# A macaron block in fp32 on one core: weight sums of the second feed-forward made during the mixer and kept in DRAM, buffers given by due time, and the head in one list

## The chip, the cores and the metric

The kernel runs on one core of one Trainium2 chip. The metric is the device time of one execution in microseconds (us): 2007.45 us as the median of three runs (2005.02 to 2007.62) for the kernel before.

## What is computed

For 256 tokens of width 2048, all in fp32, three sublayers stand in a row, each between two norms and with a residual:

```
...
for l in range(DEPTH):
    f = _swiglu(_rmsnorm(h, ln_ffn1_pre[l]), ffn1_gate[l], ffn1_up[l], ffn1_down[l])
    h = h + MACARON_WEIGHT * _rmsnorm(f, ln_ffn1_post[l])
    mx = _hybrid_mixer(_rmsnorm(h, ln_mix_pre[l]), w_in[l], ...)
    h = h + _rmsnorm(mx, ln_mix_post[l])
    f = _swiglu(_rmsnorm(h, ln_ffn2_pre[l]), ffn2_gate[l], ffn2_up[l], ffn2_down[l])
    h = h + MACARON_WEIGHT * _rmsnorm(f, ln_ffn2_post[l])
...
```

`_swiglu` is `(silu(x @ w_gate) * (x @ w_up)) @ w_down` with a hidden width of 5632. The mixer multiplies by `w_in`, runs a linear recurrence (RWKV-7) over 16 heads and a windowed pooling beside it, and joins both by gated products with `w_proj_a`, `w_proj_b` and `w_out`.

## The kernel before

**Matmuls.** A fp32 number is split into a high part H (a cast by ScalarE, ACT) and the rest L (a subtraction by VectorE, DVE). `mm3` (L332 to L334) makes each product as three matmuls of 128x128 by 128x512. Weights come by SP's queue in tiles of 128x1024 fp32 (512 KB, two k-tiles of 512 columns) into four `w32` buffers; `two` (L386, L396 in `fetch`, L308, L309) writes the halves into a ring of five `wH`, `wL` pairs. All other large tiles are "units" of 4 KB a partition, 33 of them in one pool (`s.unit`, NUNITS): activations, sums, scratch.

**Quads.** In the feed-forwards two outputs of 512 columns are made together, `f` and `l` (a block of gate and of up, or two column blocks of down), for the two halves of the tokens. For two k-tiles that is 2x2 by 2x2, and `seven` does it either as two plain pairs (one `f` and one `l`, 12 matmuls each) or as one quad: Strassen's seven products in Winograd's form, 21 matmuls. A quad needs four sums of weights (t13, two tiles, in L622; t2 in L627; t4 in L631) and the split of seven weight tiles (L639, L644). In the letter lists GATE_UP and DOWN, `f` and `l` are pairs, `q` is a quad whose sums are all made on DVE, and `Q` one whose t13 is made by an adding DMA of GpSimd (POOL): `begin` loads two tiles by SP, `adding` (L617) adds the third, and DVE makes t2 and t4 alone. The five PE steps of a quad are at the end of `quad`. GATE_UP has 17 q, 24 Q, 78 f and l pairs; DOWN 11 q and 7 Q. Both feed-forwards use the same lists.

**The planner.** `Plan` holds the steps of a feed-forward as nodes of an engine with a duration, dependencies, and buffers ("tokens") taken and released. `solve` gives each a due time from PE's order, simulates the engines with fixed costs, and returns one order, in which the instructions are issued by hand (`run`, inside `manual_schedule`). A unit is taken by whichever node is ready first.

**The head.** The first product starts cold: `head` writes its own order for PE, ACT, DVE and SP inside a `manual_schedule` of its own (transposes of x, splits of the first weights, L309). The plan of the first feed-forward is a second such list. It begins with `normed`, which joins H and L of the activations (L1249).

**The mixer.** Only PE has an order by hand there; the other engines are ordered by the compiler's scheduler, by place in the program, with weight splits boosted ahead. It opens with plain products by `tok_g`: each loops over k-tiles, four at a time (three where it is 288 columns wide). The opening is one group of 288 columns and five of 512 (two for the pooling, then k, v and r of the first half of the heads). Then two recurrences, one for each half, are woven with more such products ("fill": the other half's k, v, r, the gates, `w_proj_b`). `across` moves the results into place with 16 small POOL transfers each (L1071). In the opening, `uT2` holds 8 units, `R` 15, `lq` and `sgb0` one each.

Of the kernel before, what the change touches and what calls it, by code (L numbers as in the profile page):

```python
# [10 lines left out]
F32 = mybir.dt.float32  # L11
# [6 lines left out]
P = 128  # L18
# [26 lines left out]
DOWN = ((0, "fffffQfffQfffflfqllQlllqqllQlqllflll", 0),  # L45
        (2, "fQqffqfqllffQqflffqfQfqlqf", TRAIL))
OUT = ((0, "", 0), (1, "fffqfq" "qlqlll", 0), (3, "", TRAIL))
GATE_UP = ["", "fffflQlfqfllll",
           "fqqflQQQfll", "flflQfqqQfll", "flqQfffqQlll",
           "flfQfQqfqlll", "flffQQqqQll", "fQfQfQQfllll",  # L50
           "ffqqQflQqll", "flffQQqfQlll", "fQfqqlQlflfl"]
SUMS = (2, 2, 1)
LATE, KEPT = 7, 5
# [30 lines left out]
class Node:  # L84
    def __init__(s, eng, dur, fn, deps, take, rel, due, size, ahead, spare, lat, early):
        s.eng, s.dur, s.fn, s.due, s.size = eng, dur, fn, due, size
        s.early = early
        s.ahead, s.spare, s.lat = ahead, spare, LAT[eng] if lat is None else lat
        s.deps = [d for d in deps if d]
        s.take, s.rel = take, rel  # L90
        s.start = s.end = s.free = None
        for r in rel:
            r.left += 1


class Plan:


    def __init__(s):
        s.fifos = {r: [] for r in FIFO}  # L100
        s.nodes, s.last, s.chain, s.clk = [], None, {}, 0.0
        s.units, s.inserts = [0.0] * UNITS["out"], []
        s.begin = s.pe(BEFORE, lambda: None)
# [39 lines left out]
    def solve(s):  # L143
# [15 lines left out]
        busy = dict.fromkeys(LAT, 0.0)  # L159
# [3 lines left out]
        ready = {}  # L163

# [26 lines left out]
        while len(order) < len(s.nodes):  # L191
# [15 lines left out]
            when(n)  # L207
            front[n.eng].remove(n)
# [23 lines left out]
class Block:  # L232
    def __init__(s, tc, ctx):
        s.tc = tc
        s.nc = nc = tc.nc
        E = ctx.enter_context
        s.n = 0
        s.nxt = None
        s.late, s.after, s.chain_pow = [], [], None
        s.own_stats = False  # L240
        s.plan, s.ready = Plan(), {}
# [36 lines left out]

    def run(s):

        E = mybir.EngineType
# [245 lines left out]
    def seven(s, wf, cf, wl, cl, at, dep, KT, need, sm, order, ev_f, ev_l, used, trail=0):  # L527
# [4 lines left out]
        n = order.lower().count("q")  # L532
# [5 lines left out]
        early = "l" in order[:order.lower().rfind("q") + 1].lower()  # L538
# [4 lines left out]
        if n and early and trail:  # L543
            cut["l1"] = std - 2 * order[:order.lower().rfind("q")].count("l")
        if n and trail:
            cut["l0"] = std - 2 * order[:order.lower().rfind("q")].count("l")
# [44 lines left out]
        def quad(q, far):  # L591
            k = 2 * q
            v, x = {}, {}
# [52 lines left out]
            if far:  # L646
                n13 = p.op("SP", 0.8, begin, take=[k13], size=0.52, ahead=FETCH)
                n13 = p.op("POOL", 1.0, adding, [n13], size=0.94, lat=FAR)
# [15 lines left out]
            n2 = p.op("DVE", one, t2, [n13, ld[0]], [k24] * far, [ka, k13])  # L664
            lb, rb = half("b", 1, [ld[3]], [kb])
            n4 = p.op("DVE", one, t4, [n2, ld[3]], (), [kb])
# [79 lines left out]
        for c in order:  # L746
            if c in "qQ":
                last["q"] = quad(nq, c == "Q")
# [45 lines left out]
    def head(s, w, c0, KT, do, keep, xs):  # L794
# [10 lines left out]
        E = mybir.EngineType  # L805
        with s.tc.manual_schedule(engines={E.PE, E.Activation, E.DVE, E.SP}):
# [33 lines left out]
    def tok_g(s, w, c0, at, KT, evac, cw=512):  # L840
# [3 lines left out]
        for k0 in range(0, KT, n):  # L844
            for k, wH, wL in s.load_w(w, k0, min(n, KT - k0), c0, cw):
                xH, xL = at(k)
                for h in range(2):
                    s.mm3(pss[h], xH[:, h * P:h * P + P], xL[:, h * P:h * P + P], wH, wL,
                          k == 0, k == KT - 1)
                    yield 3 * MM * cw / 512  # L850
        s.prime()
        with s.tc.high_priority(offset=BOOST):
            for h in range(2):
                evac(h, pss[h])

# [224 lines left out]
    def ffn(s, wg, wu, wd, uT, rs, gpost, resid, emit, reload, xs=None):  # L1080
# [3 lines left out]
        nb = NKF // 4  # L1084
        one = cost("DVE", 512)
# [23 lines left out]
        p.units = UNITS["first" if xs else "ffn"]  # L1109
        rsd = p.begin  # L1110
# [54 lines left out]
        su, sud, suk = [None] * 6, {}, []  # L1165

        def need(q):
            j = q // 2
            if j not in sud:
                sud[j], k = s.sums(nT, nTd, j, su, nq=SUMS[j], x32=nx[j])  # L1170
# [3 lines left out]
        for b in range(1, nb):  # L1174
# [9 lines left out]
            def ev_l(h, d, ap, use, b=b, silu=silu, mul=mul, k1=k1):  # L1184
                g, mine = silu[h]

                def mult():
# [8 lines left out]
                    GATE_UP[b], ev_f, ev_l, {})  # L1196
            carry(b, [mul[0], mul[1]], k1)
        p.release([p.last], nTk + suk)
        s.post(wd, s.T_at(hT), NKF, gpost, 0.5, resid, emit, reload, hT, hTd, sm, DOWN, hTk, hx)
# [35 lines left out]
    def normed(s, uT, rb, rows, uTk):  # L1235
# [6 lines left out]
        for i in range(len(uT)):  # L1242
# [13 lines left out]
            def low(x=x, nH=nH, nL=nL):  # L1256
# [8 lines left out]
                             () if i < len(SUMS) else [kx]))  # L1265
            toks += kT
            if i < len(SUMS):
# [239 lines left out]
    def mixer(s, prm, uT, rs, resid, emit, gpost, reload):  # L1507
# [150 lines left out]

        with s.tc.manual_schedule(engines={mybir.EngineType.PE}):
# [3 lines left out]
            for hf in range(2):  # L1663
                weave(chain(hf), fill)
# [396 lines left out]
def kernel(tc, x, ln_ffn1_pre, ln_ffn1_post, ffn1_gate, ffn1_up, ffn1_down,  # L2061
# [11 lines left out]
    with ExitStack() as ctx:  # L2073
# [48 lines left out]
        s.mixer(prm, uT2, rs2, at_tok(h1), emit2, ln_mix_post[0],  # L2122
                load_to(h1, lambda h: hsp[0, h]))

        def emit(h, c, ap, node, t):
# [3 lines left out]
              at_tok(h2), emit, load_to(h2, lambda h: hsp[1, h]))  # L2129
# [33 lines left out]
```

## Time and profile before

| | |
|---|---|
| median of three runs | 2007.45 us (2005.02 to 2007.62) |
| the profiled execution | 2005.37 us |
| its span | 2003.7 us |
| PE busy | 1990.0 us (99%) |
| weight loads of PE | 1644.7 us (82%) |
| DVE busy | 1813.6 us (91%) |
| ACT busy | 1224.3 us (61%) |
| POOL busy | 410.0 us (20%) |
| HBM read, written | 445.45 MB, 8.39 MB |

The span is from the first to the last instruction. Busy time is the time in which an engine has an instruction of its own running. By the stages of the trace the first feed-forward ends near 700 us, the mixer's opening lies from 717 to 843 us, its recurrences end near 1180 us, and the second feed-forward begins near 1290 us (the product with `w_out` lies between). A row of a view by stage gives the stage, its length, then for PE, PEld (weight loads), DVE, ACT and POOL the busy time with the number of instructions, then the clock granted to PE, the busy share of the 16 DMA engines and the GB/s moved.

### The profile page before, as it was taken

Reading aid. Unit: us, or ns where it says so; the run is one execution under the profiler, and the core shown is the slowest. Engines: PE = TensorE matmul, PEld = TensorE weight load, DVE = VectorE, ACT = ScalarE, POOL = GpSimd, SP = SyncE. Lnnn points to the kernel's source line nnn. Section 1 sums busy time; section 2 is a strip of 40 time slices with the busy share of each in tenths; the row PEclk is TensorE's granted clock in tenths of the full one; section 3 lists DMA queues with packets and bytes.
Section 4 is the critical chain, followed back from the end, with each engine's and each line's share of the span. In section 5 each row is a group of like instructions: output and inputs, shape, how many; then the busy total and the mean of one; then the engine's idle time right before and its main releaser. Section 6 shows DMA issues by size and latency. Waiting matters only on the chain.

```text
span 2003.7 us, 29050 instructions
## 1 busy us (share of the span) xinstructions
PE 1990.0 (99%) x9903; PEld 1644.7 (82%) x9903; DVE 1813.6 (91%) x2462; ACT 1224.3 (61%) x1631; POOL 410.0 (20%) x747
## 2 busy tenths in 40 slices
PE   9999999999999999999999999999999999999998
PEld 7888888888888888888788788888888888888886
DVE  6999999999999957799689678989999999999997
ACT  7566665676665566685466434575666656666563
POOL 2222231323000113412320111012222313230000
PEclk9999999999999999999999999999999999999999
DMA  9788798878778767757556547768888988876784
GB/s 341 226 268 270 216 304 271 254 238 257 211 229 272 264 191 210 206 174 219 147 168 189 169 158 262 263 226 276 265 269 254 276 259 244 258 242 207 232 284 158
DMA packets 253941, 472.36 MB, mean 236 GB/s; under 512 B 27363, under 2 KB 30816, under 8 KB 253792
## 3 DMA queue, kind: packets, MB, share of 16 engines
q1 hardware_dynamic: 213984, 400.89, 60.4%
q0 software_dynamic: 39520, 69.08, 15.3%
q8 instruction: 78, 1.28, 0.3%
q10 hardware_dynamic: 288, 0.52, 0.1%
q14 instruction: 71, 0.58, 0.1%
HBM read 445.45 MB, written 8.39 MB: 227 GB/s over the span
## 4 chain that ended last, share of the span: by engine, by line
PE 93%; DVE 3%; DMA 2%; issue 1%; ACT 0%; SPq 0%; DVEq 0%; POOLq 0%; POOL 0%; ACTq 0%
PE mm L332 25%; PE mm L334 24%; PE mm L333 24%; PE ms L333 5%; PE ms L334 5%; PE ms L332 5%; DMA w<-in_ffn_down_dram 1%; DVE wL L644 1%; PE tr L939 1%; DVE wL L396 1%; DMA w<-in_w_out_dram 0%; PE pA L1881 0%; DVE t L622 0%; PE mc L901 0%; DVE t L627 0%
## 5 line engine op out<-in xcount | busy, mean ns | idle before, releaser
L332 PE MATMUL mm<-wH,xH 128*128 128x512 f32 (+1 forms) x2008 | 784.3, 391 | 2.0 <-ACT wH L386 1.5
L334 PE MATMUL mm<-wH,xL 128*128 128x512 f32 (+1 forms) x2008 | 779.4, 388 | 0.1
L333 PE MATMUL mm<-wL,xH 128*128 128x512 f32 (+1 forms) x2008 | 779.3, 388 | 0.1
L332 PEld LDWEIGHTS mm<-wH,xH 128*128 128x128 f32 x2008 | 377.2, 188 | 80.9 <-ACT wH L386 1.9
L334 PEld LDWEIGHTS mm<-wH,xL 128*128 128x128 f32 x2008 | 377.0, 188 | 78.7 <-DVE xL L957 1.1
L333 PEld LDWEIGHTS mm<-wL,xH 128*128 128x128 f32 x2008 | 377.3, 188 | 75.7 <-DVE wL L309 0.4
L639 ACT CAST wH<-t 128x1024 fp32r<-128x1024 f32 x244 | 257.1, 1055 | 221.2 <-PE mm L334 121.0
L386 ACT CAST wH<-w 128x1024 fp32r<-128x1024 f32 x293 | 302.8, 1053 | 128.6 <-PE mm L334 100.8
L396 DVE TENSOR_TENSOR wL<-w,wH 128x1024 fp32r<-128x1024 f32 x293 | 351.9, 1227 | 13.8 <-ACT wH L386 12.5
L644 DVE TENSOR_TENSOR wL<-t,wH 128x1024 fp32r<-128x1024 f32 x244 | 295.7, 1234 | 10.9 <-ACT wH L639 10.2
L309 DVE TENSOR_TENSOR wL<-w,wH 128x1024 fp32r<-128x1024 f32 (+2 forms) x184 | 217.5, 1190 | 84.6 <-ACT wH L308 83.2
L308 ACT CAST wH<-w 128x1024 fp32r<-128x1024 f32 (+2 forms) x184 | 188.8, 1030 | 167.0 <-PE mm L334 147.5
L639 ACT CAST wH<-w 128x1024 fp32r<-128x1024 f32 x244 | 200.1, 837 | 109.7 <-PE mm L334 75.1
L982 POOL DMA_DIRECT2D x<-T x352 | 180.6, 608 | 389.6 <-DVE T L965 76.1
L644 DVE TENSOR_TENSOR wL<-w,wH 128x1024 fp32r<-128x1024 f32 x244 | 231.6, 966 | 0.9 <-ACT wH L639 0.9
L333 PE MATMUL ms<-wL,sH 128*128 128x512 f32 x312 | 121.5, 389 | 0.2 <-DVE wL L644 0.2
L332 PE MATMUL ms<-wH,sH 128*128 128x512 f32 x312 | 121.4, 389 | 0.0
L334 PE MATMUL ms<-wH,sL 128*128 128x512 f32 x312 | 121.4, 389 | 0.0
L617 POOL DMA_DIRECT2D t<-in_ffn_up_dram x48 | 59.8, 1256 | 230.8 <-DMA t<-in_ffn_up_dram 56.1
L631 DVE TENSOR_TENSOR t<-w,t 128x512 f32<-128x512 f32 x122 | 85.5, 701 | 0.5 <-DMA w<-in_ffn_down_dram 0.2
L627 DVE TENSOR_TENSOR t<-w,t 128x512 f32<-128x512 f32 x122 | 85.3, 700 | 0.3 <-DMA w<-in_ffn_down_dram 0.3
L622 DVE TENSOR_TENSOR t<-w,w 128x1024 f32<-128x1024 f32 x60 | 73.8, 1231 | 2.8 <-DMA w<-in_ffn_down_dram 2.8
(353 smaller groups left out, 2312.4 us busy)
## 6 DMA issues: line engine op xcount, KB each, us to landing
w<-in_w_in_dram SPq DMA_DIRECT2D x128, 512.0 KB, 4.3
w<-in_ffn_down_dram SPq DMA_DIRECT2D x104, 512.0 KB, 6.5
w<-in_ffn_up_dram SPq DMA_DIRECT2D x94, 512.0 KB, 6.0
w<-in_ffn_gate_dram SPq DMA_DIRECT2D x92, 512.0 KB, 6.6
w<-in_ffn_gate_dram SPq DMA_DIRECT2D x168, 256.0 KB, 5.5
w<-in_ffn_down_dram SPq DMA_DIRECT2D x130, 256.0 KB, 4.9
w<-in_ffn_up_dram SPq DMA_DIRECT2D x116, 256.0 KB, 5.9
t<-in_ffn_up_dram POOLq DMA_DIRECT2D x48, 512.0 KB, 8.4
```

What stands on the lines that cost most here:

```text
L308: s.nc.scalar.copy(vH, v)
L309: s.nc.vector.tensor_tensor(out=vL, in0=v, in1=vH.bitcast(F32), op=ALU.subtract)
L332: nc.tensor.matmul(ps, aH, bH, start=start, stop=False, skip_group_check=seeded)
L333: nc.tensor.matmul(ps, aH, bL, start=False, stop=False, skip_group_check=seeded)
L334: nc.tensor.matmul(ps, aL, bH, start=False, stop=stop, skip_group_check=seeded)
L386: nc.scalar.copy(x["H"], x["v"])
L396: nc.vector.tensor_tensor(out=x["L"], in0=x["v"], in1=x["H"].bitcast(F32), op=ALU.subtract)
L627: V.tensor_tensor(out=v["t24"][:, 0], in0=v["a"][:, 0], in1=v["t13"][:, 1], op=ALU.add)
L631: V.tensor_tensor(out=v["t24"][:, 1], in0=v["b"][:, 1], in1=v["t24"][:, 0], op=ALU.add)
L639: nc.scalar.copy(H, src)
L644: V.tensor_tensor(out=L, in0=src, in1=H.bitcast(F32), op=ALU.subtract)
L982: nc.gpsimd.dma_start(out=x[0][q * 32:q * 32 + 32, i], in_=src[i * 32:i * 32 + 32, q])
```

## The change

1. **Sums made in the mixer.** The second feed-forward has lists of its own, GATE_UP2 (17 q, 8 Q, 23 of a new letter P, 64 pairs) and DOWN2 (9 q, 9 Q): 66 quads in place of 59. For each P, `premakes` loads four weight tiles into two units, makes t13, t2 and t4 with three DVE adds into a third unit and in place, and stores them to a DRAM tile by two POOL transfers. In `tok_g` one such job is taken after the k-tiles 4, 8 and 12 of a product, in the mixer's opening and during the second recurrence (PRE_AT). In the second feed-forward a P loads its two tiles of sums by SP (`bring`) in place of making them.
2. **Buffers by due time.** In `solve`, a node that takes units leaves free as many as the nodes due before it still need (`kept_for`). The lists of the first feed-forward are written anew for it, with the same number of quads (18 q and 23 Q in gate and up, 11 q and 7 Q in down).
3. **Head in one list.** `head` leaves its `manual_schedule` open and `run` goes on in it, with POOL among the listed engines from the start; the plan counts DVE as taken for its first 5.5 us and ACT for 4.5 us (TAKEN).

```
+GATE_UP2 = ["", "fPllfPfPqfll",
+    "flffPqPlfqll", "fqqPllqPffl", "fPfqPlPqlfl",
+    "fqfqPQflPll", "fflqQQPQfll", "fPqPllQPffl",
+    "fqfqlQQfPll", "flPPflqPqfl", "fPlqQPPlffl"]
+DOWN2 = ((0, "ffffffQfffflQqflllfqQlqlllQllQlfflll", 0),
+    (2, "fqffqQflqflQflqqqfffflQfQf", TRAIL))
+TAKEN = dict(DVE=5.5, ACT=4.5)
+PRE = 0
+PRE_AT = ((4, 8, 12), (), (4, 8, 12))
...
-        busy = dict.fromkeys(LAT, 0.0)
+        busy = {**dict.fromkeys(LAT, 0.0), **s.taken}
...
+        def kept_for(n):
+            c = 0
+            for m in takers:
+                if m.due >= n.due or c > NUNITS:
+                    break
+                c += m.units
+            return c
...
+            aside = kept_for(n) if any("unit" in k.res for k in n.take) else 0
...
-                    u, i = free[k.res[1]], HOLD if r == "ring" else SPARE
+                    u = free[k.res[1]]
+                    i = max(aside + (r == "ring"), HOLD if r == "ring" else SPARE)
...
-                at = free[r][i] if len(free[r]) > i else 1e18
+                j = i + aside * (r == "unit")
+                at = free[r][j] if len(free[r]) > j else 1e18
...
-        with s.tc.manual_schedule(engines={E.PE, E.Activation, E.DVE, E.SP, E.Pool}):
+        with s.open or s.listed():
+            s.open = None
             for n in s.plan.solve():
...
+            def bring(i):
+                v[("t13", "t24")[i]] = s.unit((P, 2, 512), F32, ("t13", "t24")[i])
+                nc.sync.dma_start(out=v[("t13", "t24")[i]], in_=made(q)[:, i])
+            if ready_made:
+                n13, n4 = [p.op("SP", 0.4, lambda i=i: bring(i), take=[(k13, k24)[i]], size=0.52,
+                                ahead=FETCH) for i in range(2)]
+            elif far:
...
+            if not ready_made:
+                n2 = p.op("DVE", one, t2, [n13, ld[0]], [k24] * far, [ka, k13])
...
+            if not ready_made:
+                n4 = p.op("DVE", one, t4, [n2, ld[3]], (), [kb])
...
-        with s.tc.manual_schedule(engines={E.PE, E.Activation, E.DVE, E.SP}):
+        stack = ExitStack()
+        stack.enter_context(s.listed())
+        with stack:
...
+            s.open = stack.pop_all()
...
+            if k0 in s.pre_at:
+                with s.tc.high_priority(offset=-PRE):
+                    next(s.jobs, None)
...
+    def premakes(s, wg, wu):
...
+                k = 2 * q
+                out = s.made[b, q] = s.dp.tile([P, 2, 2, 512], F32, tag=f"made{b}_{q}",
+                                               name=f"made{b}_{q}")
+                x, y, t = [s.unit((P, 2, 512), F32, n_) for n_ in ("ma", "mb", "mt")]
+                for i in range(2):
+                    for v, w in ((x, (wg, wu)[i]), (y, (wu, wg)[i])):
+                        nc.sync.dma_start(out=v[:, i], in_=w[(k + i) * P:(k + i + 1) * P,
+                                                             b * 512:b * 512 + 512])
+                V = nc.vector
+                V.tensor_tensor(out=t, in0=x, in1=y[:, :1].to_broadcast([P, 2, 512]), op=ALU.add)
+                V.tensor_tensor(out=y[:, 0], in0=x[:, 0], in1=t[:, 1], op=ALU.add)
+                V.tensor_tensor(out=y[:, 1], in0=y[:, 1], in1=y[:, 0], op=ALU.add)
+                nc.gpsimd.dma_start(out=out[:, 0], in_=t)
+                nc.gpsimd.dma_start(out=out[:, 1], in_=y)
+                yield
...
+        s.pre_at = PRE_AT[0]
         with s.tc.manual_schedule(engines={mybir.EngineType.PE}):
...
             for hf in range(2):
+                s.pre_at = PRE_AT[1 + hf]
                 weave(chain(hf), fill)
...
+        s.jobs = s.premakes(ffn2_gate[0], ffn2_up[0])
```

More of the change, by code (lines that the diff above doesn't have):

```diff
@@ L91, in __init__ @@
         s.start = s.end = s.free = None
+        s.units = 0
         for r in rel:
@@ L163, in solve @@
         ready = {}
+        takers = sorted((n for n in s.nodes if any(k.res[0] == "unit" for k in n.take)),
+                        key=lambda n: n.due)
+        for n in takers:
+            n.units = sum(k.res[0] == "unit" for k in n.take)
         def add(n):
@@ L207, in solve @@
             when(n)
+            if n.units:
+                takers.remove(n)
             front[n.eng].remove(n)
@@ L240, in __init__ @@
         s.own_stats = False
-        s.plan, s.ready = Plan(), {}
+        s.plan, s.ready, s.open = Plan(), {}, None
+        s.made, s.jobs, s.pre_at = {}, iter(()), ()
         s.cp = E(tc.tile_pool(name="cp", bufs=1))
@@ L525, in sums, with seven @@
         return d, kept
-    def seven(s, wf, cf, wl, cl, at, dep, KT, need, sm, order, ev_f, ev_l, used, trail=0):
+    def seven(s, wf, cf, wl, cl, at, dep, KT, need, sm, order, ev_f, ev_l, used, trail=0,
+              made=None):
         nc, p = s.nc, s.plan
         V = nc.vector
-        n = order.lower().count("q")
+        n = sum(order.count(c) for c in "qQP")
         K0 = 2 * n
@@ L537, in seven @@
         left = dict(f0=std + n, f1=std + n, l0=std + n, l1=std, p1=n, p5=n, p6=n, p7=n)
-        early = "l" in order[:order.lower().rfind("q") + 1].lower()
+        last_q = max(order.rfind(c) for c in "qQP")
+        early = "l" in order[:last_q + 1].lower()
         ready = [[], []]
@@ L746, in seven @@
         for c in order:
-            if c in "qQ":
-                last["q"] = quad(nq, c == "Q")
+            if c in "qQP":
+                last["q"] = quad(nq, c == "Q", c == "P")
                 nq += 1
@@ L854, in tok_g @@
                 evac(h, pss[h])
+    def premakes(s, wg, wu):
+        nc = s.nc
+        for b, order in enumerate(GATE_UP2):
+            quads = [c for c in order if c in "qQP"]
+            for q, c in enumerate(quads):
+                if c != "P":
+                    continue
+                k = 2 * q
[13 more added lines that the diff above has]
+                yield
+        yield True
     def prime(s):
@@ L1109, in ffn @@
         p.units = UNITS["first" if xs else "ffn"]
+        p.taken = TAKEN if xs else {}
         rsd = p.begin
```

45 lines of the change are left out of this document (24 added, 21 removed).

## The prediction

> **What bounds the kernel now.** I read the page first (busy times and the chain that ended last), then the busy times by stage, then the few stages in which TensorE (PE) is not full, instruction by instruction. The page:
>
> ```profile
> span 2003.7 us, 29050 instructions
> PE 1990.0 (99%) x9903; PEld 1644.7 (82%) x9903; DVE 1813.6 (91%) x2462; ACT 1224.3 (61%) x1631; POOL 410.0 (20%) x747
> PE 93%; DVE 3%; DMA 2%; issue 1%; ACT 0%; SPq 0%; DVEq 0%; POOLq 0%; POOL 0%; ACTq 0%
> ```
>
> PE is busy for all but 13.7 us of the span, and the chain of waits is 93% PE. So a change gains only by fewer matmuls or by less of those 13.7 us, and loses by any new wait of PE. Two full stages, one in each feed-forward (columns: stage, length, then busy time and count of PE, weight loads, DVE, ACT, POOL, clock, DMA share, GB/s):
>
> ```profile
> 200.00:300.00 100.00, 100.00 (x443) 82.81 (x442) 99.16 (x118) 62.25 (x68) 26.84 (x45) 1.00 0.90 259
> 1400.00:1500.00 100.00, 100.00 (x443) 82.84 (x442) 99.93 (x122) 62.86 (x70) 23.39 (x38) 1.00 0.88 271
> ```
>
> 443 matmuls in 100 us: one of 512 columns costs PE 0.2257 us, at the full clock. DVE stands right behind PE, at 99 to 100%: what limits the number of quads in these stages is DVE. Where PE's 13.7 us lie:
>
> ```profile
> 20.00:25.00 5.00, 5.00 (x26) 4.13 (x25) 3.10 (x8) 3.63 (x10) 0.00 (x0) 1.00 1.06 385
> 25.00:30.00 5.00, 3.51 (x18) 2.52 (x16) 5.00 (x7) 3.89 (x8) 0.00 (x0) 1.00 1.05 387
> 30.00:35.00 5.00, 4.88 (x21) 3.87 (x21) 5.00 (x9) 5.00 (x12) 0.00 (x0) 1.00 1.05 387
> ...
> 40.00:45.00 5.00, 5.00 (x24) 4.13 (x23) 2.67 (x4) 2.20 (x3) 4.66 (x27) 1.00 1.01 326
> ...
> 1990.00:2004.00 14.00, 4.84 (x22) 3.68 (x20) 3.65 (x6) 0.69 (x2) 0.54 (x1) 0.83 0.32 109
> ```
>
> 9.2 us are the tail, which the change leaves alone; 1.49 + 0.12 = 1.61 us lie in one gap of the head. What made that gap, from the instructions of PE and DVE in order of time:
>
> ```profile
> 27.84 0.40 PE L332 MATMUL mm<-wH,xH 128*128 128x512 f32 x1
> 29.73 0.50 PE L332 MATMUL mm<-wH,xH 128*128 128x512 f32 x1 [1.49 <-ACT wH L386]
> ```
>
> ```profile
> 25.68 3.49 DVE L1249 TENSOR_TENSOR nx<-xH,xL 128x1024 f32<-128x1024 f32 x3
> 29.08 1.22 DVE L309 TENSOR_TENSOR wL<-w,wH 128x1024 fp32r<-128x1024 f32 x1
> ```
>
> Three joins of the plan (L1249), which nobody needs yet, ran on DVE ahead of a weight split of the head (L309). PE had no second half of the weights until that split.
>
> **The change, part by part.**
>
> *Seven more quads in the second feed-forward.* Counting q, Q and P in the letter lists: 41 + 18 = 59 before, 48 + 18 = 66 after (23 of them P; the announced 24 I cannot find in the letters). Two pairs take 24 matmuls; a quad, by its five PE steps, takes 6 + 3 + 6 + 3 + 3 = 21. So 7 x 3 x 0.2257 = **4.74 us less** of PE.
>
> *Does DVE allow it?* The stage of the second gate and up products, and its DVE rows (mean ns of one after the busy time):
>
> ```profile
> 1290.00:1690.00 400.00, 399.69 (x1780) 331.39 (x1781) 385.98 (x484) 250.28 (x315) 95.47 (x159) 1.00 0.83 258
> ```
>
> ```profile
> L396 DVE TENSOR_TENSOR wL<-w,wH 128x1024 fp32r<-128x1024 f32 x80 | 96.2, 1231 | 4.8 <-ACT wH L386 4.6
> L644 DVE TENSOR_TENSOR wL<-t,wH 128x1024 fp32r<-128x1024 f32 x69 | 83.9, 1239 | 0.0
> L644 DVE TENSOR_TENSOR wL<-w,wH 128x1024 fp32r<-128x1024 f32 x70 | 66.6, 972 | 0.2 <-ACT wH L639 0.2
> L627 DVE TENSOR_TENSOR t<-w,t 128x512 f32<-128x512 f32 x36 | 25.4, 706 | 0.0
> L631 DVE TENSOR_TENSOR t<-w,t 128x512 f32<-128x512 f32 x35 | 24.7, 707 | 0.0
> L622 DVE TENSOR_TENSOR t<-w,w 128x1024 f32<-128x1024 f32 x15 | 18.5, 1238 | 0.0
> ```
>
> A pair costs DVE 1.23 us. Every quad has four subtractions, 2 x 1.24 + 2 x 0.97 = 4.42; a P has nothing else; a Q adds 0.71 + 0.71 (5.83); a q adds 1.24 more (7.07). Gate and up before: 17 q, 24 Q, 78 pairs = 120.2 + 139.9 + 95.9 = 356.0 us. After: 17 q, 8 Q, 23 P, 64 pairs = 120.2 + 46.6 + 101.7 + 78.7 = 347.2. In the down product two q become Q, 2.5 less. DVE loses 11.3 us where PE loses 4.7, so it falls further behind PE and the 7 quads are covered, at no cost. If the planner's times were wrong there, PE would wait, which it now does for 0.31 of these 400 us; I bound that by the 4.74 itself.
>
> *Transfers there.* A load of 128x512 is 0.262 MB. A q brings 4 of them, Q and P each the worth of 7 (P's two sums are 0.524 MB each), a pair 2. Together 102.7 MB before, 108.2 after, so 258 GB/s becomes some 275; the cover is the 385 GB/s of the row 20 to 25. No cost.
>
> *The first feed-forward* keeps its 59 quads; one Q becomes a q, 1.24 us more for DVE, which had 0.84 us idle in the 100 us of the row 200 to 300. There are ten such blocks to spread it over: nothing, at worst 1.24 us. The planner now sets units aside by due time; a lack of units would show as PE under 100%, and the row 200 to 300 has none. Nothing.
>
> *Head in one list.* The joins can no longer pass the head's splits, and the planner is told that DVE is taken for 5.5 us. The gap of **1.61 us** goes. What is late next: four joins of about 1.2 us stand behind the last split and ahead of the plan's first subtractions; DVE was idle for 2.3 of the 5 us from 40 to 45, so there is room for them. Between 0 and 1.61; I take all of it, since nothing else waited in the two windows.
>
> *The 23 sums made in the mixer.* Each is four loads of 0.262 MB on SP's queue, three adds on DVE (L622, L627 and L631 are the same shapes: 1.238 + 0.706 + 0.707 = 2.65 us) and two stores of 0.524 MB issued by POOL. No PE instruction is added. By the calls at k0 = 4, 8, 12, sixteen belong to the mixer's opening (the 288-column group meets only 12, five groups of 512 meet all three) and seven to the second recurrence. The opening is 717 to 843 us, the first recurrence 843 to 1010, the second 1010 to 1180:
>
> ```profile
> 717.00:843.00 126.00, 126.00 (x610) 106.96 (x609) 82.17 (x138) 77.33 (x121) 41.89 (x86) 1.00 0.74 216
> 843.00:1010.00 167.00, 167.00 (x1204) 136.48 (x1203) 140.35 (x258) 102.99 (x167) 44.50 (x79) 1.00 0.60 177
> 1010.00:1180.00 170.00, 169.60 (x1259) 138.11 (x1258) 135.31 (x247) 95.64 (x148) 26.90 (x43) 1.00 0.59 174
> ```
>
> DVE: 16 x 2.65 = 42.4 us into 43.8 idle; 7 x 2.65 = 18.6 into 34.7. It fits, barely in the opening. POOL, 32 stores by the row of the mixer's own stores, 0.556 us: 18 us into 84 idle.
>
> ```profile
> L1587 POOL DMA_DIRECT2D msp<-sgb x8: 544/555/607, 914.3 to 1070.1; - x8
> ```
>
> DMA is the tight place. Sixteen sums move 16 x 2.1 = 33.6 MB; with 216 GB/s x 126 us = 27.2 that is 60.8 MB in 126 us, 482 GB/s. The fastest stretch of this trace:
>
> ```profile
> 1920.00:1930.00 10.00, 10.00 (x46) 8.28 (x45) 8.43 (x9) 6.92 (x8) 0.00 (x0) 1.00 1.06 395
> ```
>
> So about 390 GB/s can be had and (482 - 390) x 126 us = 11.6 MB, 30 us of transfer, must go elsewhere. The Trainium skill, page "DMA: Bandwidth & Descriptors", section Bandwidth, says that between HBM and SBUF the core's HBM share of some 358 GB/s binds, not the fabric's 435. The row with 395 disagrees, and the measurement decides; by 358 the overflow would be an estimated 15.6 MB, or 44 us.
>
> Where does the overflow go? Each sum holds three units while in flight, and of 33 units uT2 holds 8, R 15, lq and sgb0 one each: 8 are left, two sums at a time, fewer once mix and z take theirs. That throttles the sums, not the weights. The first recurrence can take them: (390 - 177) x 167 us = 35.6 MB are free there. And the weights run well ahead of PE: the casts wait for PE, hardly for data.
>
> ```profile
> ACT wH L308 <- PE mm L334: 147.3, 93, 4.4
> ...
> ACT wH L308 <- DMA w<-in_w_in_dram: 5.2, 4, 1.9
> ```
>
> Four load buffers and five of the ring, each of 12 matmuls (2.71 us), are at most 24 us of PE work; less a landing and the two halves, about 18. The bounds of the cost are 0 and the overflow's 30 us; a gain is excluded, as only work is added. I take 0.5 us, near the mixer's only stall today:
>
> ```profile
> 1140.00:1160.00 20.00, 19.60 (x217) 14.97 (x214) 12.83 (x25) 6.85 (x10) 4.18 (x5) 1.00 0.43 132
> ```
>
> **Sum.** -4.74 - 1.61 + 0.5 = -5.85 us. The profiled execution took 2005.37 us (span 2003.7 and 1.7 around it), so it would be 1999.5; the median of the three runs is 2.1 higher, 2007.45, and gives **2001.6 us**.
>
> **Rivals.**
>
> *The sums stand ahead of the weights on SP (slower).* SP's queue is in order. A sum's load that waits for a unit, whose last holder is a store still landing, keeps every weight load behind it. For it: 482 GB/s against 390, and no free unit to speak of once z and mix stand. Against: the lead of 18 us, and that only 16 of them come before the first recurrence. Price: between 30 - 18 = 12 and 30 us; with 20, 2007.45 - 6.35 + 20 = 2021 us. From 6.35 + 4 = 10.4 us of new waits on it is slower, a third of the overflow.
>
> *The sums get in the recurrences' way.* What is not done by 843 us runs on DVE between the steps of the recurrence, whose PE steps wait on single DVE results:
>
> ```profile
> 880.00:900.00 20.00, 20.00 (x132) 16.06 (x130) 19.73 (x31) 13.23 (x24) 1.04 (x2) 1.00 0.58 195
> ```
>
> DVE has 0.27 us idle there. Two to four late sums of 2.65 us each that meet such steps cost 5 to 10 us: 2006 to 2011, no difference. Against it: the weight splits are boosted ahead, and PE has other products woven in.
>
> *The head's gap only moves.* Then 4.74 - 0.5 = 4.24 are left: 2003.2 us.
>
> *The quads do not come through.* The second feed-forward waits for its sums or for units, and gives the 4.74 back: 2006.3 us. Against it is DVE's 11.3 us.
>
> **How the numbers follow.** About 0.2%, 4 us, is what a measurement of this kernel can tell from no change. The forecast (all terms, new waits of up to 2.4 us) gets 0.52; the moved gap 0.11 (0.08 of it still over the bound); the recurrences 0.14; the lost quads 0.04; the queue 0.19. Faster 0.52 + 0.08 = 0.60; same 0.03 + 0.14 + 0.04 = 0.21; slower 0.19. The range goes from 1998, the forecast without any new wait less the spread of the runs (2007.45 - 6.35 - 2.4 = 1998.7), to 2014, which takes in the recurrences and the lighter end of the queue's case (2007.45 - 6.35 + 12 = 2013.1); its heavier end, 0.15, stays out. Of the likeliest case alone: 1998 to 2003.5.
>
> **What would show it.** Right: 21 matmuls fewer in all (9903 now); PE full in 25 to 35 us, with the joins behind the head's last split; 100% PE from 717 to 1180 with DVE above 95% and DMA near 390 GB/s in the opening, and sums trailing into the first recurrence; the second feed-forward 4.7 us shorter with DVE less full. Wrong: PE waiting on weight data (ACT wH for DMA w) between 720 and 860, or SP issuing weight loads late behind a sum's load; PE waiting on pA, pU or the like after 843; PE under 100% in 1290 to 1690.

## The result and the profile after

The changed kernel takes 2079.07 us (median of four runs, 2077.74 to 2080.43) beside 2007.53 us for the kernel before (four runs, 2005.02 to 2008.81): slower by a ratio of 1.0363, interval 1.035 to 1.0375. Faster was forecast; the time lies 65 us above the range. The profiled execution took 2079.83 us. Its page:

```profile
span 2077.9 us, 29451 instructions
PE 1999.4 (96%) x9882; PEld 1649.9 (79%) x9882; DVE 1860.4 (90%) x2513; ACT 1236.9 (60%) x1645; POOL 416.2 (20%) x778
PE   9999999999999999666999899999999999999998
PEclk9999999999999999777999999999999999999999
PE 83%; DVE 6%; DMA 5%; issue 4%; ACT 2%; POOL 0%; SPq 0%; DVEq 0%; POOLq 0%; ACTq 0%
```

PE has its 21 matmuls less (9882), and yet it is busy 9.4 us longer and idle for 78.5 us in place of 13.7. The rows of slices put most of that in one place, slices 17 to 19 of 40, where the granted clock falls too. Two transfers mark the stages: the first store of the first feed-forward's result and the first of the mixer's (first and last start at the end of each row). Before:

```profile
L2110 POOL DMA_DIRECT2D hsp<-fg x8: 539/542/594, 685.3 to 699.8; - x8
L2120 POOL DMA_DIRECT2D hsp<-fg x8: 539/540/593, 1305.0 to 1320.1; - x8
```

After:

```profile
L2189 POOL DMA_DIRECT2D hsp<-fg x8: 539/539/599, 683.0 to 697.5; - x8
L2199 POOL DMA_DIRECT2D hsp<-fg x8: 539/542/593, 1383.4 to 1398.5; - x8
```

| stage, us | before | after | difference |
|---|---|---|---|
| first feed-forward, to the first mark | 685.3 | 683.0 | -2.3 |
| mixer, from mark to mark | 619.7 | 700.4 | +80.7 |
| second feed-forward, to the end of the span | 698.7 | 694.5 | -4.2 |

The quads gave about what was forecast; the first feed-forward's 2.3 us are no more than its scatter over the runs (below); the mixer, priced at 0.5 us, took 80.7. The head after the change, by stage (columns as in the prediction) and then DVE in order of time:

```profile
25.00:30.00 5.00, 5.00 (x26) 4.12 (x25) 4.06 (x10) 3.88 (x8) 0.00 (x0) 1.00 1.05 386
30.00:35.00 5.00, 5.00 (x24) 4.14 (x23) 5.00 (x5) 5.00 (x12) 0.00 (x0) 1.00 1.05 385
```

```profile
28.72 1.22 DVE L343 TENSOR_TENSOR wL<-w,wH 128x1024 fp32r<-128x1024 f32 x1
29.85 1.23 DVE L1326 TENSOR_TENSOR nx<-xH,xL 128x1024 f32<-128x1024 f32 x1
```

The gap is closed: the joins stand behind the head's last split. And PE is full in the second gate and up products (400.00 of 400 us). The mixer's bad stretch, after:

```profile
820.00:840.00 20.00, 19.12 (x83) 15.16 (x82) 15.31 (x24) 9.75 (x14) 11.14 (x23) 1.00 1.05 365
840.00:860.00 20.00, 14.07 (x60) 10.87 (x59) 14.19 (x24) 9.82 (x16) 8.98 (x18) 0.91 1.05 351
860.00:880.00 20.00, 8.88 (x28) 7.22 (x28) 11.14 (x21) 10.20 (x15) 6.11 (x5) 0.57 0.84 287
880.00:900.00 20.00, 6.35 (x18) 4.58 (x19) 8.19 (x15) 8.08 (x19) 2.70 (x6) 0.57 0.73 251
900.00:920.00 20.00, 20.00 (x109) 17.20 (x108) 13.57 (x20) 10.65 (x14) 0.67 (x2) 1.00 0.61 186
920.00:940.00 20.00, 7.90 (x35) 6.20 (x33) 11.31 (x14) 6.69 (x11) 2.15 (x5) 0.76 1.00 371
940.00:960.00 20.00, 7.46 (x44) 6.52 (x45) 18.37 (x32) 9.99 (x28) 0.90 (x2) 0.56 0.09 38
```

PE has 83.8 us of work in these 140. DMA is full up to 860 us, so bytes are a suspect; but from 860 to 900 no engine is full, nor is DMA: something is awaited. After 940 DMA is nearly idle, and PE waits for steps of DVE (busy 18.37 of 20 us). What PE waits for in the mixer (total, times, longest):

```profile
PE pA L1960 <- DVE R L1936: 24.6, 1, 24.6
PE pV L1897 <- DVE zv L1582: 14.0, 3, 13.1
PE pn L1877 <- issue: 12.9, 1, 12.9
PE mm L366 <- ACT sga L1594: 6.1, 1, 6.1
```

In the mixer of the kernel without sums (e1 below) the longest row is this:

```profile
PE pA L1960 <- DVE R L1936: 1.2, 2, 1.1
```

The first three rows after the change are the first steps of the recurrence, and they want z: pn starts as soon as ACT has a square made from zk (869.5 us), pV takes zv, and pA takes what DVE makes behind zr. (sga is a gate's tile, at 1189 us.) The tiles zk, zv and zr are k, v and r, mixed with their shifted selves by ACT (L1579) into a unit each. ACT in order of time, ahead of zr:

```profile
843.68 1.26 ACT L1135 ACTIVATE R<-mm,rs 128x512 f32<-128x512 f32 x2
...
885.37 1.70 ACT L1579 ACTIVATE zv<-R,omu 128x256 f32<-128x256 f32 x4 [9.64 <-DMA made<-mt]
...
928.97 1.04 ACT L342 CAST wH<-w 128x1024 fp32r<-128x1024 f32 x1 [0.32 <-DMA w<-in_w_proj_b_dram]
936.24 1.70 ACT L1579 ACTIVATE zr<-R,omu 128x256 f32<-128x256 f32 x4 [6.23 <-DMA made<-mb]
```

The product r left PSUM at 844 us (L1135). Its shift ran at 936, and at the end it waited for `made<-mb`: the store of a sum, which holds the unit that zr is to get. Ahead of it in ACT's queue zv had waited for another such store. These two waits, 15.9 us, are all that ACT spends on stores of sums up to zr; for the rest zr stands behind other work of ACT, much of it casts of weights for later products, in the order that the compiler gave. The same two steps before the change:

```profile
841.78 0.69 ACT L1060 ACTIVATE R<-mm,rs 128x512 f32<-128x512 f32 x1 [2.54 <-PE mm L334]
...
859.12 0.50 ACT L1502 ACTIVATE zr<-R,omu 128x256 f32<-128x256 f32 x1
```

### The profile page after: what moved, and what is told of

Same layout as the page of the kernel before. It is cut to its first block, busy times and chain, and to the rows that moved or that the text cites. A ratio compares the mean times of both kernels' runs of the same rounds, so it can differ in the third digit from the quotient of the medians.

```text
span 2077.9 us, 29451 instructions
## 1 busy us (share of the span) xinstructions
PE 1999.4 (96%) x9882; PEld 1649.9 (79%) x9882; DVE 1860.4 (90%) x2513; ACT 1236.9 (60%) x1645; POOL 416.2 (20%) x778
## 4 chain that ended last, share of the span: by engine, by line
PE 83%; DVE 6%; DMA 5%; issue 4%; ACT 2%; POOL 0%; SPq 0%; DVEq 0%; POOLq 0%; ACTq 0%
PE mm L366 21%; PE mm L368 21%; PE mm L367 21%; PE ms L366 5%; PE ms L367 5%; PE ms L368 5%; DMA w<-in_w_in_dram 2%; DVE wL L343 1%; DMA mb<-in_ffn_up_dram 1%; ACT wH L342 1%; PE tr L1014 1%; DMA w<-in_w_out_dram 1%; PE pA L1960 0%; DMA ma<-in_ffn_up_dram 0%; DMA made<-mb 0%
## 5 line engine op out<-in xcount | busy, mean ns | idle before, releaser
L367 PE MATMUL mm<-wL,xH 128*128 128x512 f32 (+1 forms) x1966 | 766.9, 390 | 1.7 <-DVE wL L343 1.7
L368 PE MATMUL mm<-wH,xL 128*128 128x512 f32 (+1 forms) x1966 | 766.7, 390 | 0.7 <-DVE xL L1032 0.7
L367 PEld LDWEIGHTS mm<-wL,xH 128*128 128x128 f32 x1966 | 371.5, 189 | 77.2 <-DVE wL L343 3.6
L676 ACT CAST wH<-t 128x1024 fp32r<-128x1024 f32 x258 | 271.6, 1054 | 216.3 <-DVE t L668 90.7
L420 ACT CAST wH<-w 128x1024 fp32r<-128x1024 f32 x279 | 288.0, 1052 | 114.5 <-PE mm L368 90.0
L430 DVE TENSOR_TENSOR wL<-w,wH 128x1024 fp32r<-128x1024 f32 x279 | 333.4, 1218 | 18.4 <-ACT wH L420 17.2
L681 DVE TENSOR_TENSOR wL<-t,wH 128x1024 fp32r<-128x1024 f32 x258 | 310.0, 1218 | 3.4 <-ACT wH L676 1.8
L343 DVE TENSOR_TENSOR wL<-w,wH 128x1024 fp32r<-128x1024 f32 (+2 forms) x184 | 217.6, 1189 | 88.5 <-ACT wH L342 87.6
L676 ACT CAST wH<-w 128x1024 fp32r<-128x1024 f32 (+1 forms) x258 | 211.3, 836 | 108.5 <-PE mm L368 79.5
L681 DVE TENSOR_TENSOR wL<-w,wH 128x1024 fp32r<-128x1024 f32 (+1 forms) x258 | 241.9, 952 | 1.1 <-ACT wH L676 1.1
L654 POOL DMA_DIRECT2D t<-in_ffn_up_dram x31 | 37.5, 1208 | 554.7 <-DVE wL L681 359.2
L668 DVE TENSOR_TENSOR t<-w,t 128x512 f32<-128x512 f32 x106 | 72.6, 685 | 0.2
L664 DVE TENSOR_TENSOR t<-w,t 128x512 f32<-128x512 f32 x106 | 72.5, 685 | 0.0
```

What stands on the lines that cost most here:

```text
L343: s.nc.vector.tensor_tensor(out=vL, in0=v, in1=vH.bitcast(F32), op=ALU.subtract)
L367: nc.tensor.matmul(ps, aH, bL, start=False, stop=False, skip_group_check=seeded)
L368: nc.tensor.matmul(ps, aL, bH, start=False, stop=stop, skip_group_check=seeded)
L420: nc.scalar.copy(x["H"], x["v"])
L430: nc.vector.tensor_tensor(out=x["L"], in0=x["v"], in1=x["H"].bitcast(F32), op=ALU.subtract)
L664: V.tensor_tensor(out=v["t24"][:, 0], in0=v["a"][:, 0], in1=v["t13"][:, 1], op=ALU.add)
```

## The experiments

The first theory was that sums hold the units that z needs. Its rivals: place and priority of the sums, their bytes, and the in-order queues in which they stand. "Mixer" below is the stage from mark to mark, "zr" the start of zr's first shift counted from the mixer's first mark. Where sums are made there are 23 of them; where an expectation says 24 it follows the words of the change. Where no ratio is given, the kernel ran once; e1's eleven times lie within 5.0 us.

**e1: all but the sums.** The second feed-forward takes the first one's lists, with 59 quads and no P.

```
-PRE_AT = ((4, 8, 12), (), (4, 8, 12))
+PRE_AT = ((), (), ())
...
-  ..., cfg=(GATE_UP2, DOWN2, SUMS2))
+  ...)
```

> Only the head in one list and the buffers by due time stay; no sums are made in the mixer, and the second feed-forward takes the first one's new lists (59 quads, no P). If all of the loss comes from making the sums in the mixer, this is the head's 1.6 us faster than the kernel before: some 2006 us. If the new buffer rule or the new lists of the first feed-forward share in the loss, it is over 2010 us and PE is under 100% somewhere from 35 to 690 us.

2007.38 us against 2006.78, ratio 1.0006 (0.9997 to 1.0015). First feed-forward 683.0, mixer 623.2, second 698.8. Head and due order alone change nothing that can be measured. This mixer is the measure for the runs below.

**e2: the sums are made, but not read** (the second feed-forward has the lists of e1).

> The 23 sums are made and stored as in the changed kernel, but the second feed-forward takes the first one's lists (59 quads, no P) and never reads them. If the loss lies in making them, the time is the changed kernel's plus the seven quads, 2079 + 5 = some 2084 us. If reading them back in the second feed-forward costs (loads of sums that land late), it falls to about 2010 us.

2080.9 us, mixer 697.1. The loss lies in making the sums.

**e3: two units a sum.** The additions go in place, into the two loaded units (four of 512 columns in place of three).

```
-  x, y, t = [s.unit((P, 2, 512), F32, n_) for n_ in ("ma", "mb", "mt")]
+  x, y = [s.unit((P, 2, 512), F32, n_) for n_ in ("ma", "mb")]
...
```

> The changed kernel with each sum made in place in two units in place of three (four adds of 512 columns, same loads and stores, same values but for their place). Theory of the units: the sums hold units that z, mix and yb of the opening wait for; with a third fewer held, the loss of 72 us falls by a third or more, to under 2055 us. Theory of the DMA engines: the same 48 MB go through at the same places, and the time stays within 8 us of 2079.

2064.25 us, mixer 682.9: 17.5 us less with the same bytes, between the two forecasts. The sums do not hold a third less: with three units `ma` is free once the second addition has read it, with two both units are held until their stores land.

**e4: the sums put last by priority** (PRE = 4000 in place of 0).

> PRE from 0 to 4000: every instruction of the sums goes to the scheduler with a lower priority, so weight loads, moves and the recurrence's own steps stand ahead of them in each queue, at the same bytes and the same units. Theory of the order (SP, POOL and DVE run in order, and the sums stand ahead of what PE needs): most of the 72 us goes, to under 2020 us, with the sums trailing into later stages. Theory of the DMA engines alone: the bytes are as many, PE still waits for weights in the opening, over 2040 us.

2081.59 us, mixer 699.9. Priority alone does nothing, as the sums hardly moved: the first load of the first sum goes at 717.2 us and of the sixteenth at 930.7, after the change at 716.1 and 927.5. So their places in the queues are not tested by this run. The likely reason, not shown, is that a sum depends on nothing but free units, and where one is free it goes ahead of work that is not ready yet, whatever its rank.

**e5: a quarter of the bytes.** Loads, additions and stores over 32 of 128 rows; the number of units and instructions as it was; not read.

```
-  nc.sync.dma_start(out=v[:, i], in_=w[(k + i) * P:(k + i + 1) * P,
+  nc.sync.dma_start(out=v[:32, i], in_=w[(k + i) * P:(k + i) * P + 32,
...
```

> Sums unused, and each made of 32 of the 128 rows alone: the same instructions, DVE times, queue entries and three units a sum, but 12 MB through the DMA engines in place of 48 (283 GB/s in the opening). Theory of the DMA engines: the 73 us go, under 2015 us. Theory of the units and queues: at least half stays, over 2043 us.

2059.34 us, mixer 675.3: 21.8 less than e2. With a quarter of the bytes 52.1 of 73.9 us stay. Nor need the 21.8 be bytes alone: a store of a sum lands after 3.7 us in place of 6.5 (medians), so units are held for less time too.

**e6: no stores** (both transfers to DRAM left out; not read).

> Sums unused, loaded and added in full but never stored: 24 MB in place of 48 (349 GB/s in the opening), and the units come free after the adds. Theory of the DMA engines: 349 is under 390 GB/s, so most goes, under 2020 us. Theory of the units: the wait of zv and zr was for a store's end, so it goes as well; if this is fast and the quarter of the rows is slow, it is the units' time and not the bytes.

2051.11 us, mixer 666.5. A unit is free as soon as the last addition has read it: 30.6 us less than e2, with half of its bytes. Both theories had put it under 2020 us; 43.3 us of the loss stay.

**e7: calls spread, two units** (PRE_AT = ((8,), (4,), (4, 12)), so that fewer sums fall into the opening).

> Two units a sum, and PRE_AT = ((8,), (4,), (4, 12)): one sum for each product of the opening (5 in place of 16, 299 GB/s), the rest in both recurrences, where the DMA engines have over 200 GB/s free. Theory of the DMA engines: the opening's loss goes; what is left is some us in the recurrences, 2002 to 2012 us. Theory of the units: the recurrences hold every one of the 33 units, so sums there make yT, sc and z wait: over 2025 us.

2050.97 us, ratio 1.0225 (1.0195 to 1.0254). zr is nearly on time (184.7), and the mixer is still 671.7: the stalls now lie in the recurrences (PE is idle for 5 to 11 us in each stretch of 78 us from 839 to 1229).

**e8: eleven sums in the opening, three units** (PRE_AT = ((4, 12), (), (4, 8, 12))).

> The changed kernel with PRE_AT = ((4, 12), (), (4, 8, 12)): 11 sums in the opening in place of 16, 12 in the second recurrence in place of 7, three units each. The opening then asks for 399 GB/s, just what the DMA engines give. Theory of the DMA engines: most of the opening's 56 us of PE idle goes, under 2035 us. Theory of the units: a sum still holds three of the few free units, so the waits of zv and zr stay, over 2050 us.

2068.87 us, mixer 688.0: over 2050 us, as forecast of the units.

**e9, e10: tiles of their own.** The sums get two tiles outside the pool, 256 columns at a time, paid for by one of four w32 buffers. e10 is the control without sums.

```
+        s.op = E(tc.tile_pool(name="op", bufs=1))
-  x, y = [s.unit((P, 2, 512), F32, n_) for n_ in ("ma", "mb")]
+  for c in (0, 256):
+      x, y = [s.op.tile([P, 2, 256], F32, tag=n_, name=s.nm(n_)) for n_ in ("ma", "mb")]
...
-W32_BUFS = 4
+W32_BUFS = 3
```

> All 24 sums are made and read, but in two tiles of their own (2 KB of a partition each, 256 columns at a time), so a sum never holds a unit of the pool and only one is in work at a time; one w32 buffer of four pays for the tiles. If units held by the sums are the main cause, the z tiles follow their group's evacuation by about 20 us as before the change, the mixer's 80.7 us shrink to those of its bytes and of the missing w32 buffer, under 25 us, and the time is 2003 to 2028 us. If the bytes or the in-order queues are the main cause, the mixer stays 50 us or more behind, and the time is above 2050 us.

> The control of the run with tiles of their own: no sums, and three w32 buffers in place of four. If the fourth w32 buffer is worth little, 2006 to 2012 us; what it comes to above 2007.4 us is the price of the buffer and is taken off the other run.

e9: 2149.24 us, ratio 1.0705 (1.0685 to 1.0724), above 2050 us, as the theory of bytes and queues had it, but not in the mixer, which takes 638.3 us, 14.7 over e10's. SP's queue in e9 says where:

```profile
13.18 2.40 SPq L329 DMA_DIRECT2D w<-in_ffn_up_dram  x3
16.56 0.34 SPq L922 DMA_DIRECT2D ma<-in_ffn_gate_dram  x1
```

With free tiles the first sum starts at 17 us, among the weights of the first feed-forward, which takes 793.3 us in place of e10's 696.7. So it was the pool that had kept the sums in the mixer. e10: 2032.84 us; a w32 buffer is worth 25 us, 13.7 of it in the first feed-forward, but its mixer takes 623.6, as e1's.

**e12: the own tiles held back to the mixer**, by a copy that writes both tiles from the mixer's input ahead of the first sum.

```
+        for n_ in ("ma", "mb"):
+            nc.vector.tensor_copy(out=s.op.tile([P, 2, 256], F32, tag=n_, name=s.nm(n_))[:, 0, :8],
+                                  in_=uT[-1][1][:, 3, S - 8:].bitcast(F32))
```

> The sums in two tiles of their own as in e9, but the two tiles are first written by a copy that reads the last piece of the mixer's input, so that no sum can start in the first feed-forward as they did in e9. All 24 sums with all their bytes then lie in the mixer and in the opening of the second feed-forward, and none holds a unit. The mixer of the control with three w32 buffers took 623.6 us. If the units are the main cause, the mixer takes 635 to 655 us (the 12 half sums that e9 had in its mixer cost 14.7 us) and the first feed-forward is back at about 697 us. If the bytes and queue places are the main cause, the mixer takes 685 us or more, as far behind its control as the changed kernel is behind the kernel before.

2126.43 us, mixer 708.7: 85.1 over its control. That is the number expected of bytes and queue places, though no unit is held; zr comes at 194.1 (control 176.4). What SP and ACT waited for there:

```profile
SPq L925 <- DMA made<-ma: 119.4, 29, 13.4
...
SPq L925 <- DMA made<-mb: 22.9, 18, 2.9
```

```profile
ACT wH L343 <- DMA w<-in_w_in_dram: 119.8, 66, 8.0
```

SP stood 142 us before loads of a sum, until the store out of the same tile had landed, and the weights stood behind (in e10 ACT waited 55.7 us for those of w_in). As a test of the units alone e12 fails: it brought a queue in their place.

**e15, e16: SP and then VectorE cleared.** e15 issues the loads of e12's sums from POOL (`nc.gpsimd.dma_start`); e16 makes the additions there too (`nc.gpsimd.tensor_tensor`).

> As e12, but the loads of the sums are issued from POOL, as their stores are, so that no load of a weight stands behind them on SP. In e12 SP stood 142 us before a load of a sum (for the store out of the one tile to land) and ACT waited 120 us for weights of w_in. If that queue place is what cost e12's mixer 85 us over its control of 623.6 us, the mixer takes 630 to 660 us now. If VectorE's 71 us before the additions or the bytes are the cause, it stays above 680 us.

> As the run before, and the additions are POOL's too, so that VectorE waits for no load of a sum. If VectorE's in-order queue is the larger part of e12's 85 us, the mixer comes down to 630 to 650 us here and not in the run before; if POOL's own work (the means, the powers, the stores of the recurrence) then stands behind the sums, it stays above 680 us.

2111.41 and 2108.4 us; mixers 679.8 and 675.4, e16's between its two forecasts e15's just under the upper one. The sums also move back: of their 92 stores 84 fall into the mixer in e12, 70 in e15 and 64 in e16, the rest into the second feed-forward, which gets 8.1 and then 2.8 us longer. So SP's queue was worth 28.9 us of e12's mixer, but 15.0 of the run, and VectorE's cannot be told from nothing: a sum in the mixer (four stores) costs 4.1 us in e12, 3.2 in e15 and 3.2 in e16. In e16 51.8 us stay with zr on time (178.5). The Trainium skill, page "Trainium Kernel Development and Optimization", section Key Constraints, says that issuing from several engines saves only issue time. Here it saved 15.0 us of the run, of work that had stood behind the waiting loads.

**e17, e18: the same two steps with units** (from e3).

> The form with two units (e3, mixer 682.9 us), loads issued from POOL. In e3 the loads of the sums waited on SP about 25 us in all, so little is to be had if SP's queue is the cause there: 675 to 685 us for the mixer if the units are what costs, under 660 us if SP's queue is.

> The form with two units, loads, additions and stores all on POOL. The units are held as in e3 or longer, since POOL's additions take longer than VectorE's. If the units are the cause, the mixer stays at 675 us or more; if VectorE's queue is, it falls under 660 us.

2090.11 and 2154.07 us; mixers 708.9 and 772.6, both worse than e3's 682.9 and e17's outside both forecasts. With units, clearing the queues does not help; what delays a sum keeps its units longer. ACT's waits in e18:

```profile
ACT zk L1581 <- DMA made<-ma: 40.1, 1, 40.1
ACT zv L1581 <- DMA made<-ma: 17.0, 1, 17.0
```

Set side by side, the kernels that take units from the pool in the opening give one line (us, differences against e1's zr of 177.6 and mixer of 623.2). The last row is an estimate from their traces: the time for which the opening's sums (sixteen, in e8 eleven) hold units, each unit from its first load or write to its last read or to the landing of its store, at the run's median of store times, in unit-us:

| | e6 | e8 | e5 | e3 | e2 | change | e4 | e17 | e18 |
|---|---|---|---|---|---|---|---|---|---|
| zr later by | 42.1 | 46.3 | 49.5 | 61.0 | 74.2 | 75.6 | 78.0 | 88.3 | 132.7 |
| mixer longer by | 43.3 | 64.8 | 52.1 | 59.7 | 73.9 | 77.2 | 76.7 | 85.7 | 149.4 |
| units held | 480 | 500 | 570 | 750 | 740 | 760 | 750 | 840 | 1330 |

The product r leaves PSUM between 156 and 171 us in all of them (156 in e1), and the moves that follow it on POOL start between 159 and 173 (159 in e1). But for e8 and e18, the lateness of zr is the mixer's loss to within 3 us; and in all nine zr is late by 8 to 11% of the time for which units are held. Bytes do not order the line: six of the nine move the same, and e5 moves half of what e6 does and is later. e7 (7.1 and 48.5) and e16 (2.1 and 51.8 against its control) are off this line: there the sums spare the opening or its units, and the loss comes from elsewhere.

**e11: the head alone** (no sums, no due order: `kept_for` finds no takers; the new lists of the first feed-forward stay).

> No sums, no memory in due order: only the head in one list. If the 3.5 us that the mixer gave back in the run without sums come from the memory in due order, the head's 2.3 us stay and the time is 2004 to 2005.5 us (ratio 0.9985 to 0.999). If they come from the shifted order behind the head itself, the time is 2006.5 to 2008 us, the same as before.

2006.02 us against 2007.21, ratio 0.9996 (0.9987 to 1.0005): too small to be told from nothing, between its two forecasts, and the lowest median of all versions.

**e13: seven sums, late.** The new lists in panels 1, 3 and 5 alone, PRE_AT = ((), (), (8, 12)), two units; a version meant to gain.

> A version meant to gain: the new lists in panels 1, 3 and 5 of the gate and up products alone, which hold 7 of the 24 sums and 4 of the 7 added quads; the 7 sums are called in the second half of the mixer alone, in the form with two units. The four quads give back 4 x 0.677 = 2.7 us in the second feed-forward; the head is as in the change. If the seven sums find free units after the recurrences, the time is 2003 to 2007 us; if they hold up the second recurrence or the weights behind it, 2010 to 2025 us.

2022.42 us, ratio 1.0079 (1.0062 to 1.0096). Mixer 630.0, 6.8 over e1; a stage of e13 behind the recurrences:

```profile
1080.00:1120.00 40.00, 38.75 (x182) 31.31 (x182) 35.95 (x70) 15.10 (x18) 4.56 (x7) 1.00 1.00 360
```

Here the sums meet full DMA (1.00, 360 GB/s). The second feed-forward takes 709.2 us, since the mixed lists overload DVE (198.4 of 200 us busy from 1400 to 1600, and PE 196.1).

**e14: 66 quads, no sums.** Every P of the lists becomes a Q.

> The 66 quads without any sum in the mixer: each of the 24 quads that read a sum from DRAM makes it where it is used (the form whose first sum is an adding DMA). The mixer is then that of e1, 623 us. In the second feed-forward VectorE gets two additions of about 0.6 us for each of 24 quads, 28.8 us on top of the 657.8 us that it had after the change, 686.6 of 694.5 us. If VectorE still has room, the time is 2003 to 2006 us; if it has become the bound there, the second feed-forward takes 700 us or more and the time is 2009 to 2025 us, and the sums of the mixer were the price of the seven quads.

2033.89 us; the second feed-forward takes 724.2 in place of e1's 698.8. A stage of e14:

```profile
1400.00:1500.00 100.00, 97.74 (x420) 77.47 (x419) 99.46 (x120) 57.41 (x66) 5.93 (x5) 1.00 0.74 227
```

DVE is full and PE runs 420 matmuls in 100 us in place of 443: the seven quads do need the sums.

## Why the prediction was wrong

- **Seven more quads, -4.74.** Right: 21 matmuls fewer, the second feed-forward 4.2 us shorter (693.5 to 694.6 us in the seven kernels with these lists and four w32 buffers, 698.5 to 700.2 in the six with 59 quads).
- **DVE covers them; transfers there cost nothing.** Right: PE was full in those 400 us at 265 GB/s, and e14 shows DVE as the limit.
- **The first feed-forward, nothing; the head, -1.61.** The gap closed. The stage became 2.3 us shorter in this execution, but it ends between 683.0 and 686.3 in the runs that share its code, and e11 cannot tell the gain from nothing. The size stays open.
- **The sums, +0.5, bounds 0 to 30.** This step failed. "That throttles the sums, not the weights" counted z and mix among those that take units, but let only the sums wait for them and looked behind the sums only for the weights. But z, one unit for each of k, v and r, is due just then, and it waits for units that the sums hold. In place of 0.5 us the mixer took 77.2 more than e1's. What a sum holds follows below the list.
- **The bound of 30 us** was transfer alone. It left out how long a sum holds what others need, and what PE loses while its order stands still. In the mixer after, against e1, PE was idle 61.9 us longer and busy 15.3 us longer with the same matmuls.
- **"The weights run well ahead."** Not so: in the changed mixer ACT waited 66.0 us for weights of w_in, in that of e1 6.3. What that cost is not separated from the units: in e10 ACT waited 55.7 us for them, and its mixer is as long as e1's.
- **The rivals.** "The sums get in the recurrences' way" had the right victim, with DVE as the cause and 5 to 10 us. "The sums stand ahead of the weights on SP" named the wait for a unit whose holder's store is still landing, but on SP's queue, not on ACT's, and ended at 30 us. With units, clearing SP gained nothing (e17); with tiles of their own it gained 15.0 us of the run. Of the prediction's signs of being wrong two came: ACT waiting for weights between 720 and 860, and PE for pA behind 843.

One sum shows what is held:

```profile
716.09 0.42 SPq L920 DMA_DIRECT2D ma<-in_ffn_gate_dram  x1
...
724.84 0.69 DVE L924 TENSOR_TENSOR mb<-ma,mt 128x512 f32<-128x512 f32 x1
...
727.57 0.54 POOL L927 DMA_DIRECT2D made<-mb  x1 [2.90 <-DVE mb L925]
```

`ma` is taken for 9 us, until the second addition has read it; `mb` for 18, until its store lands (6.9 us, median); `mt` for 8: 36 unit-us. The later sums take up to 67, and the sixteen some 760, of the 8 x 126 = 1008 that the prediction's eight free units have in the opening. Nor do they stay in it: the eighth is stored at 839 us, the sixteenth at 940, and between these times z wants its units.

So the loss of the changed kernel is the lateness of z, by the line of nine kernels and by what PE waits for; and z is late, as far as these runs show, because the sums hold units. For that speak the waits on `made` and the row of units held, above all e3, e17 and e18: the same form, the same bytes and r's moves as early, while the holding grows from 750 to 1330 unit-us. Not shown is why the compiler put z as late in ACT's queue as it did: the direct waits are 15.9 us of 75.6 in the changed kernel and 64.2 of 132.7 in e18. A larger pool wasn't tried. A second cost of about 50 us appears when the opening is spared (e7, e16). Of what it is made, bytes, late weights or places in the queues of ACT, DVE and POOL, stays open. The two do not add up: all at once, they cost 77.

The sums did not pay in any form tried. They cost 77.2 / 23 = 3.4 us each in the change and 6.8 / 7 = 1.0 each at best (e13), and bring 4.2 / 23 = 0.18 us each. No version beat the kernel before by more than the noise.

## What to carry to other kernels

Price a moved piece of work by the buffers that it holds, each for the time from its first load to its last read or to the landing of its store, and set that against what the next due step needs from the same pool; free bandwidth and idle engines say nothing of that. Work without dependencies can start as soon as a buffer is free, earlier than meant (e9 at 17 us), and a low priority did not hold it back (e4). And divide first: what one moved piece can bring sets what it may cost.

## What the runs showed of the hardware

PE lost twice in a stall. In order of time, PE after the change, behind a wait of 13 us:

```profile
891.59 0.81 PE L1897 MATMUL pV<-ident,zv 128*128 128x128 f32 x2 [13.11 <-DVE zv L1582]
...
895.42 1.09 PE L1897 MATMUL pV<-ident,R 128*128 128x128 f32 x4 [1.14 <-issue]
...
897.15 0.63 PE L368 MATMUL mm<-wH,xL 128*128 128x512 f32 x1
897.58 0.63 PE L366 MATMUL mm<-wH,xH 128*128 128x512 f32 x1
...
900.11 0.39 PE L367 MATMUL mm<-wL,xH 128*128 128x512 f32 x1
900.34 0.39 PE L368 MATMUL mm<-wH,xL 128*128 128x512 f32 x1
```

At first a matmul starts every 0.43 us, from 900 us on every 0.23. The granted clock of 0.57 in these slices says the same. The Trainium skill, page "TensorE: Matmul & The Clock Gate", section Part 1: The HAM clock gate, has the clock halved after an idle window of about 3.4 us and full again after as long a busy one. The trace agrees: the matmuls are dense from 895.4 us and at full pace within 4.5 us. A stall like this therefore costs more than its length: in the changed mixer the same matmuls took 15.3 us longer.
